# Attention with the softmax's divisor on the diagonal of the turning matrix, values in runs of 512 columns, and the sink as a score column

## The chip, the cores and the metric

The kernel runs on one core of a Trainium2 chip. Its time is the device time of one launch in microseconds (us). Before the change the median of 3 runs was 1434.32 us (1434.02 to 1434.58).

## What is computed

Two layers of a trunk for 128 context tokens and 256 latent tokens of width 1024. Each layer is half a SwiGLU FFN, a mixer, half a SwiGLU FFN, and each part has an RMS norm with shift, scale and gate. Layer 0 mixes by gated linear attention and a Fourier transform. Layer 1, the one that the change touches, mixes by attention with 16 query heads over 4 key/value heads of 64 channels:

```python
def _sink_attend(q, k, v, valid, sink):
    s = jnp.einsum('bqhgd,bkhd->bhgqk', q, k).astype(jnp.float32)
    if valid is not None:
        s = jnp.where(valid, s, -jnp.inf)
    sk = jnp.broadcast_to(sink.astype(jnp.float32)[None, :, :, None, None], s.shape[:-1] + (1,))
    p = jax.nn.softmax(jnp.concatenate([s, sk], axis=-1), axis=-1)[..., :-1]
    return jnp.einsum('bhgqk,bkhd->bqhgd', p.astype(v.dtype), v)
```

Context queries see the 128 context keys. Latent queries see the 128 cached context keys and the latent keys within 128 positions. The sink is one more logit per head: it takes part in the sum of the softmax and has no value.

## The kernel before

Activations lie with channels on the partitions and the 384 tokens along the free axis (128 context, then 256 latent, in two blocks of 128). The large projections are split into a high and a low part and run as three fp32r products each (helpers `mm3x`, lines 352 to 354, and `mm3`, lines 345 to 347); the attention's own products are plain fp32.

In `mixer_swa` the attention is cut into 20 pieces, the list `todo` (line 877). A piece is `(kp, blk, g)`: `kp` is a pair of key/value heads (one on partitions 0 to 63, one on 64 to 127), `blk` a block of 128 tokens (0 context, 1 and 2 latent), `g` one of the four query head pairs. A latent piece is one head pair over 384 keys, 16 of them; a context piece is two head pairs over 128 keys, 4 of them. Tile names carry the piece: `pw013` is `kp` 0, `blk` 1, `g` 3. Each piece goes through four stages:

- `score` (lines 787 to 801): products into one of three double banks of PSUM, `banks`. For latent pieces the band of the window is added by two bf16 products with the identity (line 800).
- `probs` (lines 805 to 828): VectorE takes the maximum over the keys (816), combines it with the negated sink (817) and forms the sink's exponent (819); ScalarE takes the exponentials of each head with their sums (823, helper line 83) and that of the sink (824).
- `scale` (lines 830 to 840): VectorE adds the sink to the sums (833) and takes 1 / sum (836); the probabilities are multiplied by it, half on VectorE and half on GpSimd (840). It runs for a piece when the next piece's `probs` has been issued.
- `turn_probs` and `attend` (lines 842 to 874): six (four for a context piece) 128x128 transposes on TensorE into `banks[0]` (848), a copy to SBUF on ScalarE (850), and the products with the values, twelve instructions of 128 columns for a latent piece (870), four of 256 for a context piece (861). After the fourth head pair the result is split into `hh` and `hl`.

`step(n)` (line 890) sets TensorE's order: the scores of piece n, the turning of piece n - 3, the values of piece n - 4. TensorE's order is written by hand (`manual_schedule`) up to the last piece's scores; the order on VectorE, ScalarE and GpSimd and the tail are set by the tile scheduler. `banks[0]` takes every turning, so one piece's turning can start only when ScalarE has copied the piece before it. Around the pieces stand the rotary embedding of the last query pairs (`rope`, lines 729 to 737, on TensorE, VectorE and GpSimd) and behind them the output projection (`project_out`, lines 345 to 347).

## Time and profile before

| | before |
|---|---|
| median of 3 runs | 1434.32 us |
| the profiled execution | 1434.01 us, its span 1432.2 us |
| TensorE busy | 1405.7 us, 98% of the span |
| VectorE, ScalarE, GpSimd busy | 76%, 42%, 9% |
| share of TensorE in the chain that ended last | 96% |

The page's first part gives busy time by engine; its fourth part follows the work that ended last backwards through what released it. The attention's pieces run between 1045 and 1111 us of the span. TensorE executes every fp32 product of this kernel as two instructions, and a transpose as one; instruction counts in the rows below are those of the hardware.

### The profile page before, as it was taken

What the parts mean: (1) busy time and instruction counts of PE and PEld (TensorE: products, weight loads), DVE (VectorE), ACT (ScalarE), POOL (GpSimd) and SP (SyncE); (2) the same over time, 40 slices, a digit from 0 to 9 for tenths busy, and PEclk for the clock granted to TensorE, in tenths of its full rate; (3) what the DMA queues carried; (4) which work ended last, traced back from release to release, by engine and by line L of the source; (5) the groups of instructions that cost most, each with busy time, mean ns of one, the idle gap of its engine ahead of it and who ended that gap; (6) DMA issues with size and microseconds to landing.
All of it is one profiled execution on the core that took longest, in us unless ns stands there. A gap on an engine that the chain in (4) does not pass through costs nothing.

```text
span 1432.2 us, 21543 instructions
## 1 busy us (share of the span) xinstructions
PE 1405.7 (98%) x8512; PEld 1367.7 (95%) x8512; DVE 1088.3 (76%) x1829; ACT 599.2 (42%) x981; POOL 123.8 (9%) x97
## 2 busy tenths in 40 slices
PE   6999999999999999999999999999999999999996
PEld 5999999999889999999999999999976999999996
DVE  3899989879876888888869988885687676666433
ACT  4544343435344444343344434333357443444332
POOL 2000000102102000000100000010146200000001
PEclk9999999999999999999999999999999999999999
DMA  9666666563414456656646655665420244333331
GB/s 394 253 215 210 213 198 246 204 223 108 155 45 148 143 195 208 203 178 226 214 162 208 213 209 183 204 213 181 146 89 2 103 141 154 136 130 130 121 103 44
DMA packets 48515, 245.26 MB, mean 171 GB/s; under 512 B 5376, under 2 KB 9856, under 8 KB 29088
## 3 DMA queue, kind: packets, MB, share of 16 engines
q1 hardware_dynamic: 44560, 240.80, 48.3%
q10 hardware_dynamic: 3856, 3.10, 0.7%
q8 instruction: 66, 1.08, 0.3%
q14 instruction: 33, 0.27, 0.1%
HBM read 241.79 MB, written 2.10 MB: 170 GB/s over the span
## 4 chain that ended last, share of the span: by engine, by line
PE 96%; DMA 2%; DVE 1%; ACT 0%; issue 0%; SPq 0%; DVEq 0%; ACTq 0%
PE ffn_p L352 17%; PE ffn_p L354 17%; PE ffn_p L353 17%; PE ffn_acc L345 9%; PE ffn_acc L346 9%; PE ffn_acc L347 9%; DMA raw_mod<-in_modw 2%; PE out_acc L345 2%; PE out_acc L347 2%; PE out_acc L346 2%; PE av L870 1%; PE attn L797 1%; PE attn L352 1%; PE attn L848 1%; PE attn L353 1%; PE attn L354 1%
## 5 line engine op out<-in xcount | busy, mean ns | idle before, releaser
L211 ACT CAST whi<-raw 128x1024 fp32r<-128x1024 f32 (+2 forms) x317 | 324.6, 1027 | 606.5 <-PE ffn_p L353 285.5
L212 DVE TENSOR_TENSOR wlo<-raw,whi 128x1024 fp32r<-128x1024 f32 (+2 forms) x317 | 378.6, 1197 | 164.2 <-ACT whi L211 163.4
L352 PE MATMUL ffn_p<-hh,whi 128*128 128x388 f32 x1408 | 478.4, 340 | 3.0 <-ACT whi L211 3.0
L354 PE MATMUL ffn_p<-hh,wlo 128*128 128x386 f32 x1408 | 475.1, 337 | 0.3 <-DVE wlo L212 0.2
L353 PE MATMUL ffn_p<-hl,whi 128*128 128x384 f32 x1408 | 472.5, 336 | 0.0
L149 DVE SCALAR_TENSOR_TENSOR junk<-modw,cb 128x1024 f32<-128x1024 f32 x256 | 314.4, 1228 | 2.1
L352 PEld LDWEIGHTS ffn_p<-hh,whi 128*128 128x128 f32 x1408 | 265.3, 188 | 4.3 <-ACT whi L211 3.3
L354 PEld LDWEIGHTS ffn_p<-hh,wlo 128*128 128x128 f32 x1408 | 265.9, 189 | 1.5 <-DVE wlo L212 1.5
L353 PEld LDWEIGHTS ffn_p<-hl,whi 128*128 128x128 f32 x1408 | 264.8, 188 | 0.5
L345 PE MATMUL ffn_acc<-gh_ffn,whi 128*128 128x384 f32 x704 | 237.0, 337 | 0.8 <-DVE x L400 0.8
L347 PE MATMUL ffn_acc<-gh_ffn,wlo 128*128 128x384 f32 x704 | 236.9, 337 | 0.0
L346 PE MATMUL ffn_acc<-gl_ffn,whi 128*128 128x384 f32 x704 | 236.9, 336 | 0.0
L201 POOL TENSOR_TENSOR ssq_n<-ssq_n,sq_n 128x384 f32<-128x384 f32 x42 | 59.1, 1408 | 891.6 <-ACT sq_n L200 867.3
L345 PEld LDWEIGHTS ffn_acc<-gh_ffn,whi 128*128 128x128 f32 x704 | 132.8, 189 | 1.2 <-DVE x L400 1.2
L347 PEld LDWEIGHTS ffn_acc<-gh_ffn,wlo 128*128 128x128 f32 x704 | 132.7, 189 | 0.0
L346 PEld LDWEIGHTS ffn_acc<-gl_ffn,whi 128*128 128x128 f32 x704 | 132.7, 189 | 0.0
L438 DVE TENSOR_TENSOR ffn_e<-ffn_p,r_n 128x768 f32<-128x768 f32 x88 | 84.0, 955 | 49.0 <-PE ffn_p L354 48.9
L83 ACT ACTIVATE ffn_e<-ffn_e,ffn_wb 128x128 f32<-128x128 f32 (+1 forms) x176 | 70.2, 448 | 55.3 <-DVE ffn_wb L372 55.0
L212 DVE TENSOR_TENSOR gl_ffn<-ffn_e,gh_ffn 128x384 fp32r<-128x384 f32 x88 | 49.0, 557 | 36.4 <-ACT gh_ffn L211 36.2
L211 ACT CAST gh_ffn<-ffn_e 128x384 fp32r<-128x384 f32 x88 | 44.9, 512 | 58.8 <-DVE ffn_e L442 58.3
L442 DVE SCALAR_TENSOR_TENSOR ffn_e<-ffn_e,ffn_wb 128x128 f32<-128x128 f32 (+1 forms) x176 | 65.0, 412 | 0.0
L233 DVE SCALAR_TENSOR_TENSOR hl<-x,mods,hh 128x128 fp32r<-128x128 f32 (+1 forms) x96 | 57.2, 638 | 2.1 <-ACT hh L232 1.3
(260 smaller groups left out, 1251.5 us busy)
## 6 DMA issues: line engine op xcount, KB each, us to landing
raw<-in_w SPq DMA_DIRECT2D x120, 1024.0 KB, 4.8
modw<-in_modw SPq DMA_DIRECT2D x128, 512.0 KB, 3.4
raw<-in_w SPq DMA_DIRECT2D x16, 768.0 KB, 4.9
raw_mod<-in_modw SPq DMA_DIRECT2D x8, 1024.0 KB, 15.7
raw<-in_w_in SPq DMA_DIRECT2D x8, 1024.0 KB, 5.0
raw<-in_w_out SPq DMA_DIRECT2D x8, 1024.0 KB, 4.9
raw<-in_w_og SPq DMA_DIRECT2D x2, 1024.0 KB, 4.8
raw<-in_w_v SPq DMA_DIRECT2D x2, 1024.0 KB, 4.7
```

What stands on the lines that cost most here:

```text
L83: i = act.activation(out, in_, func, **kw)
L149: i = dve.scalar_tensor_tensor(junk, raw, 1.0, cb[:, c], op0=ALU.mult, op1=ALU.mult, accum_out=mods[l][v][:, d, c : c + 1])
L211: i = act.copy(hi, src).ins
L212: pace["last"] = dve.tensor_tensor(lo, src, f(hi), op=ALU.subtract).ins
L345: first = pe.matmul(out, lhsT=wh, rhs=mh, start=start, stop=False)
L346: pe.matmul(out, lhsT=wh, rhs=ml, start=False, stop=False)
L347: pace["product"] = pe.matmul(out, lhsT=wl, rhs=mh, start=False, stop=stop).ins
L352: first = pe.matmul(out[:, :TX], lhsT=wh, rhs=hh[:, k, :TX], start=(k == 0), stop=False)
L353: pe.matmul(out[:, :T], lhsT=wh, rhs=hl[:, k], start=False, stop=False)
L354: pe.matmul(out[:, :TM], lhsT=wl, rhs=hh[:, k, :TM], start=False, stop=(k == KD - 1))
L438: dve.tensor_tensor(e, pp[:, :, :T], feed.r.unsqueeze(1).broadcast_to([P, 2, T]), op=ALU.mult)
L442: dve.scalar_tensor_tensor(e[:, 1, t0:t1], e[:, 1, t0:t1], wb[:, 1, c : c + 1], e[:, 0, t0:t1], op0=ALU.add, op1=ALU.mult)
```

## The change

- The sink, divided by the scale 0.125, is written by VectorE as one more column of the scores in PSUM. The maximum and the exponentials run over 385 (context: 129) columns, so the sum holds the sink; the separate sink exponent, its subtraction and its addition are gone.
- The probabilities are not multiplied by 1 / sum. VectorE writes instead, for each head, a 128x128 matrix with 1 / sum on its diagonal (`inv`), and the transposes with the identity become plain fp32 products with that matrix.
- The turned probabilities of the four head pairs of one `(kp, blk)` are collected in one tile, `[P, 3, 2, 512]` with one buffer, and the values of all four are computed at once: twelve instructions of 512 columns in place of four times twelve of 128.
- In `step`, the values stand ahead of the turning. The scores of the fifth piece are no longer issued ahead of the first turning.

```diff
@@ probs @@
-                    s, w = s[:, :, :T].unsqueeze(1), tile_.unsqueeze(1)
-                sink = nsink[:, 2 * j0 : 2 * (j0 + n)]
+                    s, w = [v_[:, :, : T + 1].unsqueeze(1) for v_ in (s, tile_)]
+                dve.tensor_copy(s[:, :, :, P if blk == 0 else T], sinks[:, 2 * j0 : 2 * (j0 + n)].rearrange("p (g a) -> p g a", g=n))
                 mx = mw.tile([P, 2 * n], F32, tag=f"mx{n}", name=f"mx{nm}", bufs=bufs)
                 dve.reduce_max(mx.rearrange("p (g a) -> p g a", g=n), s, axis=AX.X)
-                dve.scalar_tensor_tensor(mx, mx, -PSC, sink, op0=ALU.mult, op1=ALU.min)
-                es = mw.tile([P, 2 * n], F32, tag=f"es{n}", name=f"es{nm}", bufs=bufs)
-                last = dve.tensor_tensor(es, mx, sink, op=ALU.subtract).ins
+                last = dve.tensor_scalar(mx, mx, -PSC, None, op0=ALU.mult).ins
...
-                actf(es, es, AF.Exp, "exp")
@@ scale @@
-                w, sm, es, n = unscaled.pop(0)
-                i = dve.tensor_tensor(sm, sm, es, op=ALU.add)
+                key, sm, n = unscaled.pop(0)
+                i = dve.reciprocal(sm, sm)
                 if behind:
                     after(i.ins, behind, "the next block's maxima before the sums")
-                dve.reciprocal(sm, sm)
-                for i in range(2 * n):
-                    g, par_ = divmod(i, 2)
-                    e = pool if par_ else dve
-                    e.tensor_scalar(w[:, g, par_], w[:, g, par_], sm[:, i : i + 1], None, op0=ALU.mult)
+                inv[key] = mw.tile([P, 2 * n, P], F32, tag=f"inv{n}", name=f"inv{key[0]}{key[1]}{key[2]}", bufs=4 - n)
+                dve.tensor_tensor(
+                    inv[key], ident.unsqueeze(1).broadcast_to([P, 2 * n, P]), sm.unsqueeze(2).broadcast_to([P, 2 * n, P]), op=ALU.mult
+                )
@@ turn_probs @@
-                        pe.transpose(pt[:, par_, i * P : i * P + P], w[:, par_, i * P : i * P + P], ident)
-                wt = mw.tile([P, 2, T], F32, tag="pT", name=f"pT{nm}")
-                act.copy(wt[:, :, :n], pt[:, :, :n])
+                        pe.matmul(pt[:, par_, i * P : i * P + P], lhsT=w[:, par_, i * step : i * step + P], rhs=inv[kp, blk, g][:, par_ if blk else 2 * i + par_],
+                                  start=True, stop=True, skip_group_check=True)
...
+                if g == 0:
+                    turned[kp, blk] = mw.tile([P, 3, 2, 512], F32, tag="pT", name=f"pT{kp}{blk}", bufs=1)
+                wt = turned[kp, blk]
+                act.copy(wt[:, :, :, g * P : g * P + P], pt[:, :, :n].rearrange("p a (i t) -> p i a t", i=3))
@@ attend @@
+                if blk and g < 3:
+                    return
+                n = 512 if blk else 2 * P
+                po = one_bank(f"av{kp}{blk}{g}")[:, :n]
+                for i, vv in enumerate((vc, vt[:, 1], vt[:, 2]) if blk else (vt[:, 0],)):
                     for par_, rows in enumerate(halves):
                         c0 = (2 * kp + par_) * 64
...
+                        pe.matmul(po[rows], lhsT=vv[:, c0 : c0 + 64], rhs=wt[:, i, par_] if blk else wt[:, par_],
+                                  start=(i == 0), stop=(i == 2 or blk == 0), skip_group_check=True)
@@ step @@
                 if n < len(todo) and n not in ws:
                     begin(n)
+                if 0 <= n - LAG - 1:
+                    attend(*todo[n - LAG - 1], wts_.pop(n - LAG - 1))
                 if 0 <= n - LAG < len(todo):
                     wts_[n - LAG] = turn_probs(*todo[n - LAG], ws[n - LAG])
-                if 0 <= n - LAG - 1:
-                    attend(*todo[n - LAG - 1], wts_.pop(n - LAG - 1))
...
                 queries(3, banks[1], lambda: begin(3))
-                begin(4)
```

Two places show what this does to the order. The first is TensorE in the step of the last piece, 123. Before, it holds the scores of 123 (`kc,qs`) with the band, the transposes of 120 (`ident,pw`) and the 128-column value products of 113 (`av`):

```order
L797 MATMUL attn1_9243<-kc_9010,qs_9161 128x384 x2
L800 LDWEIGHTS c_identb_9008
L800 MATMUL attn1_9243<-c_band_9006,c_identb_9008 128x128
L800 LDWEIGHTS c_identb_9008
L800 MATMUL attn1_9243<-c_band_9006,c_identb_9008 128x128
L848 MATMUL attn0_9242<-ident_75,pw120_9938 128x128 x6
L870 MATMUL av11_9960<-pT113_10023,vc_9011 64x128 x2
L870 MATMUL av11_9960<-pT113_10023,v1_9154 64x128 x4
```

After the change TensorE has in the same step, behind the turning of 113, the scores of 123, the values of the whole group 110 to 113 and the turning of 120 (a row here counts a product once; the hardware runs it as two instructions unless it is a transpose):

```order
L845 MATMUL attn0_9242<-inv113_9850,pw113_9809 128x128 x6
L799 MATMUL attn1_9243<-kc_9010,qs_9161 128x384 x2
L802 LDWEIGHTS c_identb_9008
L802 MATMUL attn1_9243<-c_band_9006,c_identb_9008 128x128
L802 LDWEIGHTS c_identb_9008
L802 MATMUL attn1_9243<-c_band_9006,c_identb_9008 128x128
L869 MATMUL av113_9918<-pT11_9835,vc_9011 64x512 x2
L869 MATMUL av113_9918<-pT11_9835,v1_9154 64x512 x4
L845 MATMUL attn0_9242<-inv120_9872,pw120_9841 128x128 x6
```

The value products have left three steps of four, where only the scores now stand between two turnings, and stand in the fourth as 512 columns ahead of the turning. The second place is ScalarE some 30 us earlier. Before, each piece's copy (`pT`, of the turning in the same step) stands ahead of the exponentials (`pw`) of that step's scores:

```order
L850 COPY pT011_9616<-attn0_9242 128x768
L83 ACTIVATE pw020_9596,sm020_9602<-attn2_9244,mx020_9597 128x384 x2
L83 ACTIVATE es020_9600<-es020_9600 128x2
L850 COPY pT012_9658<-attn0_9242 128x768
L83 ACTIVATE pw100_9636,sm100_9642<-attn1_9243,mx100_9637 128x128 x4
L83 ACTIVATE es100_9640<-es100_9640 128x4
L850 COPY pT013_9692<-attn0_9242 128x768
L83 ACTIVATE pw021_9670,sm021_9676<-attn2_9244,mx021_9671 128x384 x2
```

After the change the exponentials of a step stand ahead of its copy there (the copies into `pT01` are those of pieces 011, 012 and 013 in turn):

```order
L84 ACTIVATE pw020_9575,sm020_9580<-attn2_9244,mx020_9577 128x385 x2
L855 COPY pT01_9569<-attn0_9242 128x6x128
L84 ACTIVATE pw100_9604,sm100_9609<-attn1_9243,mx100_9606 128x129 x4
L855 COPY pT01_9569<-attn0_9242 128x6x128
L84 ACTIVATE pw021_9628,sm021_9633<-attn2_9244,mx021_9630 128x385 x2
L855 COPY pT01_9569<-attn0_9242 128x6x128
L84 ACTIVATE pw022_9657,sm022_9662<-attn1_9243,mx022_9659 128x385 x2
```

The copy that frees `banks[0]` for the next turning now waits in ScalarE's queue behind exponentials of scores that were issued just before the turning that it copies. Over the 16 pieces from 012 on this is so for ten; for 012, 102, 111, 120, 121 and 122 the copy still stands first.

## Rows read from the trace of the kernel before

**Rows 1.** The page: busy time by engine; the chain that ended last, by engine.

```profile
PE 1405.7 (98%) x8512; PEld 1367.7 (95%) x8512; DVE 1088.3 (76%) x1829; ACT 599.2 (42%) x981; POOL 123.8 (9%) x97
...
PE 96%; DMA 2%; DVE 1%; ACT 0%; issue 0%; SPq 0%; DVEq 0%; ACTq 0%
```

**Rows 2.** Windows: length, busy time (instructions) by engine, granted clock, DMA share, GB/s.

```profile
1060.25:1110.50 50.25, 49.06 (x439) 32.24 (x438) 40.32 (x116) 38.99 (x117) 28.81 (x24) 1.00 0.07 22
...
1120.00:1420.00 300.00, 299.17 (x1717) 298.58 (x1716) 169.49 (x260) 120.03 (x176) 18.87 (x13) 1.00 0.35 121
```

**Rows 3.** TensorE by line and shape: count, busy us, mean ns of one.

```profile
L848 PE MATMUL attn<-ident,pw 128*128 128x128 f32 x112 | 15.8, 275 | 0.7 <-ACT pT L850 0.7
...
L870 PE MATMUL av<-pT,v 128*64 128x128 f32 x128 | 9.7, 273 | 0.0
...
L630 PE MATMUL fb<-c_cs_s,fy 128*128 128x128 f32 x32 | 4.2, 276 | 0.0
...
L677 PE MATMUL om<-osq,ones_h 128*128 128x512 f32 x6 | 3.2, 610 | 0.2 <-ACT osq L675 0.2
```

**Rows 4.** Timeline of TensorE, one step: start us, us, instructions.

```profile
1097.82 0.92 PE L797 MATMUL attn<-kc,qs 64*128 64x384 f32 x4
1098.67 0.28 PE L800 MATMUL attn<-c_band,c_identb 128*128 128x128 bf16 x2
1098.79 0.83 PE L848 MATMUL attn<-ident,pw 128*128 128x128 f32 x6
1099.55 0.44 PE L870 MATMUL av<-pT,vc 128*64 128x128 f32 x4
1099.82 0.61 PE L870 MATMUL av<-pT,v 128*64 128x128 f32 x8
1100.36 0.92 PE L797 MATMUL attn<-kc,qs 64*128 64x384 f32 x4
```

**Rows 5.** Timeline of TensorE at other places, layer 0 first.

```profile
387.85 1.05 PE L630 MATMUL fb<-c_cs_s,fy 128*128 128x128 f32 x8
...
406.67 1.02 PE L677 MATMUL om<-osq,ones_h 128*128 128x512 f32 x2
...
1062.58 0.66 PE L848 MATMUL attn<-ident,pw 128*128 128x128 f32 x4 [0.68 <-ACT pT L850]
...
1086.57 0.61 PE L848 MATMUL attn<-ident,pw 128*128 128x128 f32 x4
```

**Rows 6.** Timeline of ScalarE in the step of rows 4.

```profile
1097.87 0.59 ACT L83 ACTIVATE pw<-attn,mx 128x384 f32<-128x384 f32 x1
...
1098.99 0.21 ACT L83 ACTIVATE es<-es 128x2 f32<-128x2 f32 x1
1099.71 0.80 ACT L850 COPY pT<-attn 128x768 f32<-128x768 f32 x1 [0.50 <-PE attn L848]
1100.41 0.59 ACT L83 ACTIVATE pw<-attn,mx 128x384 f32<-128x384 f32 x1
```

**Rows 7.** Timeline of VectorE in the same step.

```profile
1098.99 0.96 DVE L816 TENSOR_REDUCE mx<-attn 128x2 f32<-128x768 f32 x1 [0.45 <-PE attn L800]
1099.98 0.16 DVE L817 SCALAR_TENSOR_TENSOR mx<-mx,nsink 128x2 f32<-128x2 f32 x1
1100.18 0.16 DVE L819 TENSOR_TENSOR es<-mx,nsink 128x2 f32<-128x2 f32 x1
...
1100.45 0.17 DVE L836 RECIPROCAL sm<-sm 128x2 f32<-128x2 f32 x1
1100.66 0.42 DVE L840 TENSOR_SCALAR pw<-pw,sm 128x384 f32<-128x384 f32 x1
```

**Rows 8.** Timeline of VectorE where the pieces begin, and beside the rotary embedding.

```profile
1063.66 0.95 DVE L816 TENSOR_REDUCE mx<-attn 128x2 f32<-128x768 f32 x1
...
1072.35 1.23 DVE L833 TENSOR_TENSOR sm<-sm,es 128x2 f32<-128x2 f32 x1
```

**Rows 9.** Timeline of GpSimd beside the last of rows 8.

```profile
1072.29 1.27 POOL L737 TENSOR_TENSOR qs<-qs,rp2q 128x512 f32<-128x512 f32 x1
```

More of the change, by code (lines that the diff above doesn't have):

```diff
@@ L33 @@
 TH = T + 16
+SK = P + 4
 LAG = 3
@@ L725, in mixer_swa @@
             halves = (slice(0, 64), slice(64, P))
-            nsink = mp.tile([P, 16], F32, name="nsink")
-            dve.tensor_scalar(nsink, pcol("sink"), -1.0, None, op0=ALU.mult)
+            sinks = mp.tile([P, 16], F32, name="sinks")
+            dve.tensor_scalar(sinks, pcol("sink"), 1.0 / PSC, None, op0=ALU.mult)
             def rope(src, dst, nm):
@@ L791, in score @@
                         for par_, rows in enumerate(halves):
-                            pe.matmul(s[:, par_, i * P : i * P + P], lhsT=qs[rows, 4 * kp + g + i, :P], rhs=kr[rows, kp, :P],
+                            pe.matmul(s[:, par_, i * SK : i * SK + P], lhsT=qs[rows, 4 * kp + g + i, :P], rhs=kr[rows, kp, :P],
                                       start=True, stop=True, skip_group_check=True)
@@ L801, in score @@
                               start=False, stop=True, skip_group_check=True)
-            unscaled = []
+            unscaled, inv = [], {}
             def probs(kp, blk, g, s):
@@ L808, in probs @@
                 n, j0, bufs = 1 if blk else 2, 4 * kp + g, LAG + 2
[L809 removed]
+                tile_ = mw.tile([P, 2, T + 4], F32, tag="pw", name=f"pw{nm}", bufs=bufs)
                 if blk == 0:
[L811 removed]
+                    s, w = [v_[:, :, : 2 * SK].rearrange("p a (g k) -> p g a k", g=2)[:, :, :, : P + 1] for v_ in (s, tile_)]
                 else:
[L813 to L814 removed]
+                    s, w = [v_[:, :, : T + 1].unsqueeze(1) for v_ in (s, tile_)]
+                dve.tensor_copy(s[:, :, :, P if blk == 0 else T], sinks[:, 2 * j0 : 2 * (j0 + n)].rearrange("p (g a) -> p g a", g=n))
                 mx = mw.tile([P, 2 * n], F32, tag=f"mx{n}", name=f"mx{nm}", bufs=bufs)
                 dve.reduce_max(mx.rearrange("p (g a) -> p g a", g=n), s, axis=AX.X)
[L817 to L819 removed]
+                last = dve.tensor_scalar(mx, mx, -PSC, None, op0=ALU.mult).ins
                 sm = mw.tile([P, 2 * n], F32, tag=f"sm{n}", name=f"sm{nm}", bufs=bufs)
@@ L842, in turn_probs @@
+                dve.tensor_tensor(
+                    inv[key], ident.unsqueeze(1).broadcast_to([P, 2 * n, P]), sm.unsqueeze(2).broadcast_to([P, 2 * n, P]), op=ALU.mult
+                )
             def turn_probs(kp, blk, g, w):
-                nm = f"{kp}{blk}{g}"
                 pt = banks[0]
-                n = T if blk else 2 * P
+                n, step = (T, P) if blk else (2 * P, SK)
                 for par_ in range(2):
                     for i in range(n // P):
-                        pe.transpose(pt[:, par_, i * P : i * P + P], w[:, par_, i * P : i * P + P], ident)
@@ L849, in turn_probs @@
-                wt = mw.tile([P, 2, T], F32, tag="pT", name=f"pT{nm}")
-                act.copy(wt[:, :, :n], pt[:, :, :n])
+                        pe.matmul(pt[:, par_, i * P : i * P + P], lhsT=w[:, par_, i * step : i * step + P], rhs=inv[kp, blk, g][:, par_ if blk else 2 * i + par_],
+                                  start=True, stop=True, skip_group_check=True)
+                if blk == 0:
+                    wt = mw.tile([P, 2, 2 * P], F32, tag="pT0", name=f"pT{kp}{blk}{g}", bufs=1)
+                    act.copy(wt, pt[:, :, :n])
+                    return wt
@@ L859, in attend @@
                     for par_, rows in enumerate(halves):
                         c0 = (2 * kp + par_) * 64
-                        pe.matmul(po[rows], lhsT=vt[:, 0, c0 : c0 + 64], rhs=wt[:, par_, : 2 * P], start=True, stop=True, skip_group_check=True)
-                    g0 = g
-                else:
-                    if (kp, blk) not in outs:
-                        outs[kp, blk] = one_bank(f"av{kp}{blk}")
-                    po, g0 = outs[kp, blk], 0
-                    for i, vv in enumerate((vc, vt[:, 1], vt[:, 2])):
-                        for par_, rows in enumerate(halves):
-                            c0 = (2 * kp + par_) * 64
-                            pe.matmul(po[rows, g * P : g * P + P], lhsT=vv[:, c0 : c0 + 64], rhs=wt[:, par_, i * P : i * P + P],
-                                      start=(i == 0), stop=(i == 2), skip_group_check=True)
@@ L872, in attend @@
-                if blk == 0 or g == 3:
-                    heads = slice(kp * 4 + g0, kp * 4 + g + (1 if blk else 2))
-                    split(hh[:, heads, ts], hl[:, heads, ts], po.rearrange("p (g t) -> p g t", t=P))
+                        pe.matmul(po[rows], lhsT=vv[:, c0 : c0 + 64], rhs=wt[:, i, par_] if blk else wt[:, par_],
+                                  start=(i == 0), stop=(i == 2 or blk == 0), skip_group_check=True)
+                heads = slice(kp * 4, kp * 4 + 4) if blk else slice(kp * 4 + g, kp * 4 + g + 2)
@@ L876, in mixer_swa @@
+                split(hh[:, heads, ts], hl[:, heads, ts], po.rearrange("p (g t) -> p g t", t=P))
             lat = [(kp, blk, g) for kp in range(2) for blk in (1, 2) for g in range(4)]
```

8 lines of the change are left out of this document (2 added, 6 removed).

## The prediction

> **What bounds the kernel now.** I read the busy times and the chain first: TensorE is busy 98% of the span and holds 96% of the chain that ended last [rows 1]. The windows then say whether that holds where the change is: from the end of the last query projection (1060.25) to the end of the last values (1110.5) TensorE is busy 49.06 of 50.25 us at a granted clock of 1.00 (2.4 GHz), and behind it 299.17 of 300 [rows 2]. So TensorE's work in the attention stands on the path, 1.19 us of waiting is all that other work could give back there, and a later end of the attention moves the end of the kernel by the same amount. VectorE with 40.3 us and ScalarE with 39.0 have slack in the sum, though not much within a step. The timelines of one step give the parts: scores and band 0.97 us, transposes 0.76, values 0.81, together 2.54 from one start of scores to the next [rows 4].
>
> **Turning as a product.** Six transposes take 0.83 us and four 0.61, so one more costs 0.11 [rows 4, 5]. There are 112 instructions [rows 3] for 16 x 6 + 4 x 4 = 112 transposes: one each. A plain fp32 product of the same shape, 128x128 by 128 columns, stands in layer 0 at line 630: the code has 24, the trace has 32 + 16 instructions (the row of the 32 is in [rows 3]), two each, and eight take 1.05 us with 0.28 for one, which is (1.05 - 0.28) / 7 = 0.11 apart [rows 3, 5]. So a turning of a latent piece goes from 6 to 12 instructions 0.11 apart, from 0.76 to 1.42 us to the next block: 112 x 0.11 = +12.3 us on TensorE.
>
> **Values in runs of 512.** Before, six pairs of instructions, one for each half of the partitions, start 0.11 apart: eight instructions take 0.61, which is 3 x 0.11 + 0.27. The block takes 0.81 to the next scores, that is 6 x 0.11 and 0.15 that does not depend on the columns [rows 4]. For 512 columns the nearest rows are two full-width instructions that take 1.02 where one takes 0.61: 0.41 apart [rows 3, 5], about 4 x 0.11, so I take 0.43. A block is then 6 x 0.43 + 0.15 = 2.73, and about 0.1 more since TensorE now goes from the band to the half-width products and from them to the turning (a start behind a change of form comes 0.2 after the last one, not 0.11: 0.76 = 5 x 0.11 + 0.21). Per group 4 x 0.81 = 3.24 becomes 2.83; four groups give -1.6. Bounds: 0.41 a pair and no extra change of form, -2.5; the halves not side by side at 512 columns, 12 x 0.43, +8.7.
>
> The Trainium skill, page "TensorEngine Tiling (Array Packing)", section "Instruction Overhead", says that each matmul carries about 60 cycles of overhead. By it the 144 instructions that go would save 144 x 25 ns = 3.6 us. The trace does not bear it out here: starts 0.11 apart for 128 columns, against 0.41 to 0.43 for 512, leave almost nothing per instruction.
>
> **What goes elsewhere.** VectorE per piece: the exponent's subtraction, the addition and the scaling go (two small instructions of about 0.16 and one of 0.42 [rows 7]); a copy of two sink values and the diagonal (256 columns, bounded by 0.42 for 384) come. That is about even. It runs beside TensorE's step, which grows. ScalarE loses an exponent of two values, some 0.1 to 0.2 per piece. GpSimd loses its scaling, which nobody waited for long. All this I put at nothing while TensorE is the bound; if VectorE's copy to PSUM takes 0.4 instead of 0.2 it enters the waits below.
>
> **The new wait: one bank for the turnings.** A turning may start only when ScalarE has copied the last one. In the step of [rows 4, 6], the last transpose starts at 1099.35 (1098.79 + 5 x 0.11), the copy at 1099.71, and takes 0.80; so from the start of a 12-instruction turning the bank is free again after 11 x 0.11 + 0.36 + 0.80 + 0.05 = 2.44. TensorE comes back to it after 1.42 of turning and 0.97 of scores, 2.39, where values no longer stand between (before: 0.76 + 0.81 + 0.97 = 2.54 against 1.77). So the cover shrinks from 0.8 us to nothing, and a bank wait of this kind has a precedent: 0.68 at 1062.58, where two turnings followed each other [rows 5].
>
> It is worse where the exponentials stand ahead of the copy in ScalarE's queue. From a start of scores: maximum at +1.17 (1098.99 against 1097.82), here +1.37 behind the sink's copy; 0.99 to the next instruction, 0.20 until its result is used, two exponentials 1.12 (1097.87 to 1098.99), the copy 0.80, and 0.05: 4.53 [rows 4, 6, 7]. TensorE wants the bank at 0.97 + 2.39 = 3.36, so it is 1.2 late. The next such piece then starts its scores late enough to find its exponentials ready, so the loss falls on about every second one. I walked the order given for the two engines:
> - before the turning of 011: 1.7. VectorE is busy with the last query projection until 1063.66 [rows 8], and the maxima of 012 and 013 queue behind it.
> - before 013: 1.2, and up to 1.0 more, since VectorE stood still beside GpSimd's rotary product there (a sum of two columns took 1.23, to 1073.58, where GpSimd's 1.27 from 1072.29 ends) [rows 8, 9] and the maximum of 100 is scaled at that place.
> - before 100, 022 and 102: 0.4, 0.3, 0.9; the values of group 02 wait 0.2; the pieces from 111 on, whose copy stands first, 0.05 each, 0.3.
> - before 020, 021, 023, 110 and 120 none: values stand between scores and turning.
> Sum 5.0 without the rope's 1.0. That is the value taken; its ends are 0, if ScalarE's order costs nothing, and 10, if each of the ten pieces loses about a microsecond.
>
> **Sum.** +12.3 - 1.6 - 1.2 (the old waiting, whose causes are priced anew) + 5.0 = +14.5. The profiled execution took 1434.01, its span and 1.8 around it, 0.3 below the median of the runs; 1434.0 + 14.5 gives 1448.5.
>
> **Rivals.**
> - *The copies stay hidden.* Only TensorE's own work counts: +12.3 - 1.6 - 1.2 = +9.5, 1443.5. For it: ScalarE and VectorE are under 80% busy in [rows 2]. Against it: 2.44 against 2.39 leaves no cover at all.
> - *The wait grows into the bound.* Each piece with exponentials first loses its microsecond: +9.5 + 10 = +19.5, 1453.5. For it: rope and split casts on both queues; against it: the alternation above and six pieces with the copy first.
> - *512 columns break the overlap of the halves.* -1.6 becomes +8.7: 1458. Nothing in the trace shows 512 at half width; 128 columns, and the scores' 384 (four in 0.92 [rows 4], where serial ones would take over 1.2), do overlap.
> - *The product costs TensorE no more than the transpose.* Then +12.3 and most of the waits fall: -1.6 - 1.2, 1431, faster. It decides if two instructions together start 0.12 apart or less. Line 630's eight in 1.05 us speak against it, as they are the same shape and type.
> - *It costs four times a transpose.* 112 x 3 x 0.11 = +37, and the copies hidden behind it: 1434 + 37.3 - 1.6 - 1.2 = 1468.5. Against it the same rows: 0.22 a product. The Trainium skill, "TensorE: Matmul & The Clock Gate", section "Terms", gives the transpose mode as 4x faster for FP32; by that rule this rival would hold, and line 630 says 2x.
>
> **How the numbers follow.** Forecast 0.62 (its own range 1445.5 to 1451.5), hidden copies 0.17, larger wait 0.16, no overlap 0.02, free product 0.02, fourfold product 0.01. The range of 8 in 10 is from 1442.5, the hidden copies with the cheaper bound of the values (0.9 less), to 1453.5, the larger wait. Beyond 0.2% (2.9 us), about what a measurement of this kernel can tell from no change, only the free product could come near the other side: -2.8 is at the edge, so I split its 0.02. Faster 0.01, same 0.01, slower 0.98.
>
> **What would show it.** In the profile after: 224 turning instructions 0.11 apart and 1.42 per latent turning (wrong at 0.76, or far above 1.6); 48 value instructions with pairs about 0.43 apart, 2.7 to 2.9 a block; TensorE idle ahead of turnings, released by ScalarE's copy, 4 to 7 us in all, the longest ahead of 011 and 013 and little from 111 on; no loss before 1060 or behind the attention. The prediction is wrong if TensorE's busy time in the attention grows by less than 8 us, if the waits stay under 2 or go over 9, or if they name VectorE's diagonal in place of the copy.

## The result, and the profile after

The changed kernel takes 1451.53 us in the median of 4 runs (1451.48 to 1451.58), against 1434.34 before on the same chip: ratio 1.0121 [1.0108, 1.0134], 17.2 us slower. The forecast of 1448.5 was 3 us short: inside the range of 8 in 10 (1442.5 to 1453.5), and 0.03 us above the end of the narrower range that the forecast had for itself (1445.5 to 1451.5). The profiled execution took 1451.58 with a span of 1449.8, against 1434.01 and 1432.2, so the spans differ by 17.6.

From the page after, the busy times and the chain that ended last, which answer to [rows 1]:

```profile
PE 1419.8 (98%) x8480; PEld 1376.4 (95%) x8480; DVE 1085.1 (75%) x1805; ACT 598.2 (41%) x961; POOL 95.7 (7%) x73
...
PE 94%; DVE 2%; DMA 2%; ACT 1%; issue 0%; SPq 0%; DVEq 0%; ACTq 0%
```

TensorE is busy 14.1 us longer and idle 30.0 us of the span in place of 26.5. These two, 14.1 and 3.5, are the whole 17.6. VectorE and GpSimd have less work than before, and it buys nothing.

A total over the whole kernel holds one thing that no edit touched. In the first 40 us, where TensorE stands still for a third of the time, it is busy 26.49 us before, 26.24 after, and up to 27.61 in the traces of the experiments; what it is busy more there it is idle less. So the totals scatter by up to 1.4 us, and work is better compared from 1040 us on. The line before, and the one after:

```profile
1040.00:1432.20 392.20, 380.10 (x2337) 359.49 (x2336) 237.89 (x431) 173.72 (x335) 58.23 (x45) 0.99 0.31 105
1040.00:1449.80 409.80, 394.50 (x2305) 368.17 (x2303) 235.49 (x407) 172.56 (x315) 29.82 (x21) 0.99 0.29 101
```

Counted so, TensorE's work grows by 14.4 us and its idle time by 3.2.

Windows of the kernel after (length, busy time by engine with instructions, granted clock, DMA share, GB/s). The first two answer to [rows 2], the other three are one stretch inside the attention:

```profile
1060.25:1128.00 67.75, 63.16 (x410) 42.85 (x408) 37.91 (x97) 38.74 (x105) 5.08 (x4) 0.97 0.05 16
1130.00:1438.00 308.00, 307.17 (x1760) 305.63 (x1757) 173.12 (x266) 122.73 (x180) 19.28 (x13) 1.00 0.34 118
...
1075.60:1077.40 1.80, 0.03 (x1) 0.00 (x0) 1.66 (x6) 1.80 (x9) 0.00 (x0) 1.00 0.00 0
1077.40:1080.50 3.10, 3.04 (x14) 2.96 (x15) 0.44 (x1) 1.37 (x6) 0.00 (x0) 0.54 0.00 0
1080.50:1082.50 2.00, 2.00 (x10) 0.99 (x8) 0.69 (x1) 0.57 (x1) 0.85 (x1) 0.86 0.00 0
```

The attention takes 67.75 us against 50.25, and what follows runs as full as before: a plain shift. (The two stretches don't hold quite the same work: the new one ends ahead of the last values, which start at 1128.26, and holds some 23 products of the output projection where the old one holds 9. The two differences nearly cancel.) Inside, TensorE waits 4.59 us against 1.19. And there is something that the prediction did not have: after a stretch of 1.8 us with 0.03 us of work, the granted clock reads 0.54, close to the lower of its two levels (1.2 GHz of 2.4), and then 0.86 on the way back. In narrower windows the clock reads 1.00 to the end of the idle stretch and until 1077.60, when TensorE had just taken up work again, and 0.51 from there to 1081.00.

TensorE's timeline after (start us, us, instructions, and idle time before with its releaser), which answers to [rows 4]; the lines left out repeat the pattern:

```profile
1063.83 1.16 PE L845 MATMUL attn<-inv,pw 128*128 128x128 f32 x8
1064.91 0.92 PE L799 MATMUL attn<-kc,qs 64*128 64x384 f32 x4
...
1066.56 1.60 PE L845 MATMUL attn<-inv,pw 128*128 128x128 f32 x12
1068.10 0.92 PE L799 MATMUL attn<-kc,qs 64*128 64x384 f32 x4
...
1069.92 1.60 PE L845 MATMUL attn<-inv,pw 128*128 128x128 f32 x12 [0.69 <-ACT pT L855]
1071.36 1.03 PE L735 MATMUL rotq<-qs,c_rot 128*128 128x256 f32 x4
...
1075.35 0.28 PE L802 MATMUL attn<-c_band,c_identb 128*128 128x128 bf16 x2
1077.46 2.78 PE L845 MATMUL attn<-inv,pw 128*128 128x128 f32 x12 [1.82 <-ACT pT L855]
1080.03 1.54 PE L735 MATMUL rotq<-qs,c_rot 128*128 128x256 f32 x4
...
1082.57 1.08 PE L869 MATMUL av<-pT,vc 128*64 128x512 f32 x4
1083.47 1.89 PE L869 MATMUL av<-pT,v 128*64 128x512 f32 x8
1085.29 0.94 PE L845 MATMUL attn<-inv,pw 128*128 128x128 f32 x6
```

A latent turning has 12 instructions and takes 1.54 to the next block (1066.56 to 1068.10) where 0.76 stood before; a context turning takes 1.08 (1063.83 to 1064.91). The values block of 512 columns takes 2.72 (1082.57 to 1085.29). One turning, at 1077.46, took 2.78 with the same 12 instructions, and the rotary product behind it 1.54 where the one at 1071.36 took 1.03.

Why TensorE stood for 1.82 us there is read from the other engines. ScalarE's timeline after, around that place:

```profile
1075.21 0.37 ACT L84 ACTIVATE pw<-attn,mx 128x129 f32<-128x129 f32 x1 [2.56 <-DVE sm L832]
...
1076.60 0.81 ACT L855 COPY pT<-attn 128x768 f32<-128x768 f32 x1
```

VectorE's timeline in the same stretch, and under it GpSimd's:

```profile
1074.03 1.09 DVE L819 TENSOR_SCALAR mx<-mx 128x4 f32<-128x4 f32 x1
1075.03 0.15 DVE L832 RECIPROCAL sm<-sm 128x2 f32<-128x2 f32 x1
```

```profile
1073.82 1.27 POOL L739 TENSOR_TENSOR qs<-qs,rp2q 128x512 f32<-128x512 f32 x1
```

The copy that frees the turning bank (1076.60) stands behind the exponentials of piece 100; those waited for VectorE, whose scaling of four maxima took 1.09 us, where the same instruction took 0.17 at 1088.52, and ended at about 1075.1, where GpSimd's 1.27 from 1073.82 end too. (The profile names the reciprocal right behind the scaling as the releaser; the exponentials read only the maxima.) ScalarE was idle for 2.56 us, and from about 1074.5, when the turning ahead had ended, with a copy to do that its queue held back.

The waits of TensorE in the attention after (tile and line that waited, releaser: us in all, times, longest) name that copy but for one of 0.5 us, as the prediction said, and no scores:

```profile
PE attn L845 <- ACT pT L855: 3.6, 5, 1.8
PE attn L845 <- ACT pw L84: 0.5, 1, 0.5
PE av L869 <- ACT pT L855: 0.4, 1, 0.4
```

### The profile page after: what moved, and what is told of

Its sections match the earlier page's. It is cut to its first block, busy times and chain, and to the rows that moved or that the text cites. A ratio compares the mean times of both kernels' runs of the same rounds, so it can differ in the third digit from the quotient of the medians.

```text
span 1449.8 us, 21341 instructions
## 1 busy us (share of the span) xinstructions
PE 1419.8 (98%) x8480; PEld 1376.4 (95%) x8480; DVE 1085.1 (75%) x1805; ACT 598.2 (41%) x961; POOL 95.7 (7%) x73
## 3 DMA queue, kind: packets, MB, share of 16 engines
q8 instruction: 66, 1.08, 0.3%
## 4 chain that ended last, share of the span: by engine, by line
PE 94%; DVE 2%; DMA 2%; ACT 1%; issue 0%; SPq 0%; DVEq 0%; ACTq 0%
PE ffn_p L353 17%; PE ffn_p L355 17%; PE ffn_p L354 17%; PE ffn_acc L347 8%; PE ffn_acc L346 8%; PE ffn_acc L348 8%; DMA raw_mod<-in_modw 2%; PE out_acc L346 2%; PE out_acc L348 2%; PE out_acc L347 2%; PE attn L845 1%; PE av L869 1%; ACT pw L84 1%; DVE mx L818 1%; PE attn L799 0%; PE fa L623 0%
```

## The experiments

Unless it says otherwise, a ratio is to the kernel before, run on the same chip between the others. The chips differ a little: on them the kernel before took 1434.05 to 1434.48 us, so two versions are best compared by what each takes beyond its own kernel before. "The change" is the kernel of the section above.

**The product alone.** The kernel before with the diagonal matrix as the only edit:

```diff
-                for i in range(2 * n):
-                    e.tensor_scalar(w[:, g, par_], w[:, g, par_], sm[:, i : i + 1], None, op0=ALU.mult)
+                dve.tensor_tensor(inv[key], ident.unsqueeze(1)..., sm.unsqueeze(2)..., op=ALU.mult)
...
-                        pe.transpose(pt[...], w[...], ident)
+                        pe.matmul(pt[...], lhsT=w[...], rhs=inv[kp, blk, g][...], start=True, stop=True, skip_group_check=True)
```

> The kernel before with one part of the change: the transposes become fp32 products with the diagonal of 1 / sum; values by piece, the separate sink and the step's order stay as before. Theory (TensorE's own work is the cost; a turning goes from 0.76 to 1.54 us for a latent piece and from 0.54 to 1.09 for a context piece, as the profile after the change shows): 16 x 0.78 + 4 x 0.55 = +14.7 on TensorE, and as values still stand between two turnings the bank is free in time, so the waits for ScalarE's copy stay under 1.5 us in the attention and the granted clock stays at 1.00: 1447.5 to 1449.5 us. Rival (the new order of values and turnings is what costs, not the product): under 1441 us.

Measured 1449.07 us (1448.94 to 1449.16), ratio 1.0102 [1.0085, 1.0118]. TensorE's busy time is 1420.9, 15.2 more than before, of which 0.9 falls into the first 40 us; from 1040 us on it is 394.43, 14.3 more. On cost the theory holds; the rival that the order is what costs, and that of a free product, are dead. The granted clock reads 1.00 in the attention, as expected. The waits for the copy, expected under 1.5 us, were larger:

```profile
PE attn L848 <- ACT pT L851: 2.3, 4, 1.0
```

**The transposes back.** The change with the scaling and the transposes of before, and the values and the sink as changed:

```diff
-                inv[key] = mw.tile([P, 2 * n, P], F32, ...)
-                dve.tensor_tensor(inv[key], ...)
+                for i in range(2 * n):
+                    g, par_ = divmod(i, 2)
+                    e = pool if par_ else dve
+                    e.tensor_scalar(key[:, g, par_, ...], key[:, g, par_, ...], sm[:, i : i + 1], None, op0=ALU.mult)
...
-                        pe.matmul(pt[...], lhsT=w[...], rhs=inv[kp, blk, g][...], ...)
+                        pe.transpose(pt[...], w[...], ident)
```

> The changed kernel with one part undone: transposes with the identity, and the scaling by 1 / sum on VectorE and GpSimd, as before; values in runs of 512, the sink as a column and the new order stay. Theory (the product costs TensorE 14.7 us): that falls away, but TensorE then comes back to the one bank of the turnings after 0.76 + 0.97 = 1.73 us where it is free after 1.77 at best, and later behind exponentials, so the waits grow from 4.6 us to 6 to 10 us and eat the 1.6 us that the runs of 512 save: 1435 to 1440 us, not faster than before. Rival (runs of 512 and the sink's column are a gain once the product is gone): 1431 to 1433 us.

Measured 1435.22 us (1435.14 to 1435.62), ratio 1.0007 [0.9998, 1.0017]. It takes 1.0 us more than its own kernel before, so 16.2 of the 17.2 us go with the product. TensorE has 1.4 us less work than before (1404.3 busy; 1.6 less from 1040 us on) and more waits:

```profile
PE attn L799 <- ACT pw L84: 2.0, 5, 0.8
PE attn L845 <- ACT pT L854: 1.1, 1, 1.1
PE attn L845 <- ACT pw L84: 0.7, 1, 0.7
```

The saving of the runs of 512 is there and is given back: 2.0 us of these 3.8 are scores that wait for a bank whose exponentials are late, a wait that the change does not show, and that the slower turning probably covers there. Not all of it comes from the runs: the longest, 0.80 at 1067.12, has its like in the kernel with the sink column alone (below), 0.99 at 1067.44.

**The copy first.** The change with the exponentials of a step issued behind its turning:

```diff
-                ws[n] = probs(*todo[n], s)
+                return lambda: ws.update({n: probs(*todo[n], s)})
...
-                if n < len(todo) and n not in ws:
-                    begin(n)
+                then = begin(n) if n < len(todo) and n not in ws else None
...
                     wts_[n - LAG] = turn_probs(*todo[n - LAG], ws[n - LAG])
+                if then:
+                    then()
```

> The changed kernel with the exponentials of a step issued behind the turning of the same step, so that ScalarE's copy stands ahead of them in its queue; TensorE's order and all instructions are the same. Theory (TensorE waits for the bank of the turnings because the copy queues behind exponentials, and the longest wait lets the clock fall): the waits before 011, 013, 022 and 102, 0.7, 1.8, 0.6 and 0.2 us, fall to 0.3 or less each, the clock stays at 1.00 in the attention: 1446 to 1448 us. Rival (VectorE and ScalarE cannot deliver faster, whatever stands first): the waits come back under other names, 1450 us or more.

Measured 1446.61 us (1446.39 to 1446.76), ratio 1.0085 [1.0070, 1.0100]: 12.4 us more than its own kernel before, where the change takes 17.2 more. Its waits, and then its timeline of TensorE at the turning that took 2.78 us in the change:

```profile
PE attn L845 <- ACT pT L855: 1.1, 2, 0.8
PE attn L845 <- ACT pw L84: 0.5, 1, 0.5
```

```profile
1075.40 1.60 PE L845 MATMUL attn<-inv,pw 128*128 128x128 f32 x12 [0.77 <-ACT pT L855]
1076.84 1.03 PE L735 MATMUL rotq<-qs,c_rot 128*128 128x256 f32 x4
```

The wait is 0.77 and the turning takes 1.60 again; the granted clock reads 1.00 in every 10 us of the attention. Waits fell from 4.6 to 1.6, which is 3.0 us, and TensorE's busy time from 1040 us on fell by 2.1 (392.38 against 394.50), close to what the slow stretch cost. The order on ScalarE makes most of the waits, as the prediction had it. The 0.77 is more than the 0.3 that I expected to be left: one of the four exponentials of piece 100 still stands ahead of the copy in ScalarE's timeline (1074.20, the copy at 1074.56), and it waited for the same VectorE scaling of 1.09 us.

**Values by piece.** The change with 128-column values after each piece, still ahead of the turning:

```diff
-                if blk and g < 3:
-                    return
-                n = 512 if blk else 2 * P
-                po = one_bank(f"av{kp}{blk}{g}")[:, :n]
+                n = P if blk else 2 * P
+                if blk == 0:
+                    po = one_bank(f"av{kp}{blk}{g}")[:, :n]
+                else:
+                    if g == 0:
+                        outs[kp, blk] = one_bank(f"av{kp}{blk}")
+                    po = outs[kp, blk]
+                at_ = slice(g * P, g * P + P) if blk else slice(0, n)
...
-                        pe.matmul(po[rows], lhsT=..., rhs=wt[:, i, par_] ...
+                        pe.matmul(po[rows, at_], lhsT=..., rhs=wt[:, i, par_, at_] ...
...
+                if blk and g < 3:
+                    return
```

> The changed kernel with the values computed piece by piece in runs of 128 columns again, at the place in the step that they have after the change (ahead of the turning); the diagonal product and the sink's column stay. Theory (runs of 512 save 1.6 us of TensorE but uncover the bank's copy): TensorE's work grows by 1.6 us, the waits of 4.6 us fall to 2 or less and the half clock (some 1.7 us) goes: 1447 to 1449.5 us, faster than the whole change. Rival (the runs of 512 are a plain gain): 1453 us.

Measured 1452.47 us (1452.43 to 1452.49), ratio 1.0126 [1.0110, 1.0141]: a miss, on the rival's side. I had taken the values for a cover of the copy. Placed ahead of the turning they need the very copy that the turning waits for, since they read what it writes. TensorE's timeline of this kernel shows the wait in its new place:

```profile
1078.27 0.44 PE L873 MATMUL av<-pT,vc 128*64 128x128 f32 x4 [1.03 <-ACT pT L855]
...
1079.07 1.60 PE L845 MATMUL attn<-inv,pw 128*128 128x128 f32 x12
```

Its waits sum to 4.3 us, nearly those of the change, now ahead of the values. The longest is 1.03, and the clock reads 1.00 throughout. TensorE's busy time from 1040 us on is 395.49; against the change without its slow stretch (394.50 - 1.7, below) that is 2.7 more, and against the kernel with the copy first, which has no slow stretch, 3.1: nearly twice the 1.6 that I had for the runs of 512.

**Transposes and the copy first.** The two edits above together.

> The change with the four transposes and the scaling of the probabilities as they were before (1435.22 us as measured), and in each step the exps issued behind the step's turning, so that the copy out of the turning bank stands first on ScalarE. In the kernel without this reordering TensorE waits 1.1 us once in front of a turning for such a copy, 0.7 us once for exps that still read the turning bank, and 2.0 us in five places in front of scores for exps that still read their bank. Theory (the waits for the copy come from ScalarE's order): the 1.1 us go, the scores' waits stay or grow a little because every exp starts up to one copy (0.8 us) later: 1433.8 to 1435.4 us. Rival (without the dearer product there is no slack on TensorE to cover exps that start 0.8 us later, so the scores' five waits each grow): 1436 us or more.

Measured 1435.34 us (1435.14 to 1437.88), ratio 1.0006 [0.9997, 1.0015]. The number lies in the theory's range, but the run doesn't test it, because the tile scheduler, which orders ScalarE, put the exponentials ahead of the copy again. ScalarE's timeline of this kernel, at the place:

```profile
1072.99 0.37 ACT L84 ACTIVATE pw<-attn,mx 128x129 f32<-128x129 f32 x1 [0.65 <-DVE sm L832]
...
1074.38 0.81 ACT L854 COPY pT<-attn 128x768 f32<-128x768 f32 x1
```

The waits are the same three lines with the same numbers as without the edit. Inconclusive: here the order of issue was only a wish, since a scheduler decides.

**Runs of 512 alone.** The kernel before with the values of four pairs collected, turning ahead of values as before:

```diff
-                wt = mw.tile([P, 2, T], F32, tag="pT", name=f"pT{nm}")
-                act.copy(wt[:, :, :n], pt[:, :, :n])
...
+                if g == 0:
+                    turned[kp, blk] = mw.tile([P, 3, 2, 512], F32, tag="pT", name=f"pT{kp}{blk}", bufs=1)
+                wt = turned[kp, blk]
+                act.copy(wt[:, :, :, g * P : g * P + P], pt[:, :, :n].rearrange("p a (i t) -> p i a t", i=3))
...
+                    if g < 3:
+                        return
...
-                            pe.matmul(po[rows, g * P : g * P + P], lhsT=..., rhs=wt[:, par_, i * P : i * P + P],
+                            pe.matmul(po[rows], lhsT=..., rhs=wt[:, i, par_],
```

> The kernel before with one part of the change alone: values of four head pairs in one run of 512 columns, the turning ahead of the values as before, transposes and sink as before. Theory (TensorE loses 16 x 6 instruction gaps and three changes of form per group and waits for nothing new): 1.0 to 1.8 us faster, 1432.4 to 1433.3 us. Rival 1 (the one buffer for four pairs makes the first copy of a group wait for the 2.7 us of values of the group before, which now stand behind that turning, and the next turning waits for that copy, at three changes of group, about 0.7 us each): 1434 to 1436 us. Rival 2 (what was seen in the kernel with 128-column values, 3.6 us more work of TensorE, belongs to the block of 512 everywhere): 1430.5 to 1431.3 us.

Measured 1437.94 us (1437.43 to 1439.43), ratio 1.0026 [1.0015, 1.0036]: 3.5 slower, above all three ranges. The work did what the theory says (1404.2 busy, 1.5 less). Its waits in the attention:

```profile
PE attn L797 <- ACT pw L83: 1.8, 3, 1.0
PE attn L848 <- ACT pT L857: 1.7, 1, 1.7
PE attn L848 <- DVE pw L840: 1.2, 1, 1.2
PE attn L848 <- POOL pw L840: 0.8, 2, 0.5
PE attn L848 <- ACT pT L851: 0.7, 1, 0.7
```

6.2 us against 1.2 before, minus 1.5 of work, is the 3.5. The waits are of four kinds, and in this trace the single buffer of rival 1 is a small part of them at most. ScalarE's timeline at the longest, 1.66 ahead of a turning at 1082.46:

```profile
1080.39 0.58 ACT L83 ACTIVATE pw<-attn,mx 128x384 f32<-128x384 f32 x1 [2.85 <-DVE mx L817]
...
1081.61 0.80 ACT L857 COPY pT<-attn 128x768 f32<-128x768 f32 x1
```

The values that held the buffer had given it back before 1080.2; the copy started at 1081.61 because exponentials stood ahead of it. (Whether the scheduler would have put the copy first with a second buffer, no run shows.) The rest are probabilities scaled late and scores that wait for exponentials. My reading, which no run isolates, is that three steps in a row without values are shorter than VectorE and ScalarE need for a piece.

**The sink column alone.** The kernel before with the sink as a column, by the edits of `probs` and the first lines of `scale` in the diff of the change, with the layout that they need, nothing else.

> The kernel before with the sink as one more column of the scores alone: per block a copy of the sinks into the score bank (0.16 us on VectorE), the max over one column more, no exp and no sum of the sink. Theory (none of this stands on TensorE, and exps start about as late as before): within 0.6 us of before, 1433.6 to 1434.9 us. Rival (the sink's copy cannot start before the scores are written and puts 0.16 us ahead of each max, so exps and everything behind them move, 20 blocks x 0.1 to 0.16 us): 1435.5 to 1437 us.

Measured 1434.87 us (1434.42 to 1436.74), ratio 1.0005 [0.9996, 1.0014]: no difference that can be measured, as expected; TensorE's busy time is the same 1405.7. Its trace is not the same, though: scores wait 1.3 us for exponentials (0.2 before), 0.99 of it once, and the waits of TensorE in the attention sum to 2.2 us against 1.1.

**Transposes in the old order.** Values and sink as changed, transposes and scaling as before, and the order of before:

```diff
-                if 0 <= n - LAG - 1:
-                    attend(*todo[n - LAG - 1], wts_.pop(n - LAG - 1))
                 if 0 <= n - LAG < len(todo):
                     wts_[n - LAG] = turn_probs(*todo[n - LAG], ws[n - LAG])
+                if 0 <= n - LAG - 1:
+                    attend(*todo[n - LAG - 1], wts_.pop(n - LAG - 1))
...
                 queries(3, banks[1], lambda: begin(3))
+                begin(4)
```

> Values in runs of 512 and the sink column as in the change, with the four transposes, the scaling and the order of before (turning, then values; piece 4 begun ahead of the loop). It differs from the measured 1435.22 us by the order alone. Theory (the order of the change, values ahead of the turning, costs what the runs of 512 save, through waits in front of scores and turnings): 1432.0 to 1433.5 us, waits of TensorE in the attention under 2.5 us against 3.8. Rival (the single buffer of four pairs holds the first copy of the next group until the values behind the turning have run): 1434.5 to 1436 us.

Measured 1434.87 us (1434.53 to 1436.34), ratio 1.0002 [0.9993, 1.0011], above the theory's range. Its waits sum to 4.4 us, not under 2.5, of which the largest line is again scores behind exponentials (0.99 of it at the place of the wait in the kernel with the sink column alone):

```profile
PE attn L799 <- ACT pw L84: 3.0, 4, 1.2
```

With 1435.22 for the other order the order of turning and values makes no difference that can be measured here. The theory that it costs what the runs of 512 save falls.

**Filler in the wait.** The change with 14 transposes of the identity ahead of the one turning that waited 1.82 us:

```diff
+                if n - LAG == 5:
+                    fill = one_bank("fill")
+                    for _ in range(14):
+                        pe.transpose(fill[:, :P], ident, ident)
                 if 0 <= n - LAG < len(todo):
```

> The change, with 14 transposes of the identity (128x128, into a bank of their own that nobody reads) put on TensorE ahead of the turning of piece 013, in front of which TensorE waited 1.82 us in the change; at the 0.11 us that one transpose took in the trace of before they fill 1.5 us of that wait. Theory (the turning that took 2.78 us instead of 1.60, and the product behind it that took 1.54 instead of 1.03, ran slowly because the granted clock fell to 0.54 after the wait): with the wait filled the granted clock stays at 1.00 there, the turning takes 1.6 us, and the kernel is 1.4 to 1.9 us faster than the change, 1449.6 to 1450.2 us. Rival (that turning is slow for a reason of its own, its operands or its bank, and the clock reading follows from it): the turning again takes over 2.5 us, and the time is that of the change or up to 0.3 us more, 1451.4 to 1451.9 us.

Measured 1449.99 us (1449.70 to 1451.71), ratio 1.0114 [1.0098, 1.0129]: 1.5 less than the change, or 1.3 when each is set against its own kernel before (15.9 and 17.2 more), with more work in it. One of the four executions took 1451.71, as long as the change; its trace was not kept. TensorE's timeline of this kernel, and its windows over the stretches shown for the change:

```profile
1075.51 1.70 PE L897 MATMUL fill<-ident 128*128 128x128 f32 x14
1077.49 1.60 PE L845 MATMUL attn<-inv,pw 128*128 128x128 f32 x12 [0.28 <-ACT pT L855]
1078.93 1.03 PE L735 MATMUL rotq<-qs,c_rot 128*128 128x256 f32 x4
```

```profile
1075.60:1077.40 1.80, 1.61 (x16) 1.37 (x13) 1.66 (x6) 1.80 (x10) 0.00 (x0) 1.00 0.00 0
1077.40:1080.50 3.10, 3.01 (x20) 2.32 (x20) 0.91 (x2) 1.97 (x6) 0.46 (x1) 1.00 0.00 0
```

The turning starts 0.03 us later than in the change, waits for the same copy, has the same operands, and takes 1.60 in place of 2.78. At this place the theory holds: with the same wait filled, the clock stays and the turning is fast. But a wait of nearly that length need not bring the clock down. The kernels with runs of 512 alone and of 256 alone have waits of 1.66 and 1.52 us; their windows over the wait and over the work behind it:

```profile
1080.80:1082.40 1.60, 0.01 (x1) 0.00 (x0) 1.02 (x2) 1.60 (x7) 1.47 (x1) 1.00 0.00 0
1082.40:1085.50 3.10, 3.04 (x22) 1.78 (x24) 2.40 (x7) 2.80 (x13) 1.18 (x1) 1.00 0.01 3
```

```profile
1080.00:1081.50 1.50, 0.00 (x0) 0.00 (x0) 1.32 (x6) 1.28 (x6) 0.85 (x2) 1.00 0.00 0
1081.50:1084.50 3.00, 2.55 (x18) 1.29 (x18) 2.49 (x8) 2.60 (x13) 1.78 (x2) 1.00 0.01 3
```

What sets these apart from the wait of 1.82 us, the runs don't show.

**Runs of 256 alone.** The kernel before with values of two pairs in one run, two buffers. The diff is against the runs of 512 alone:

```diff
-                    turned[kp, blk] = mw.tile([P, 3, 2, 512], ..., bufs=1)
+                    turned[kp, blk] = mw.tile([P, 3, 2, 2 * P], ..., bufs=2)
...
-                    if g < 3:
+                    if g % 2 == 0:
                         return
```

> The kernel before with the values of two head pairs in one run of 256 columns in place of four in 512; two buffers for the turned probabilities of two pairs each. Theory (runs of 512 cost the kernel before 3.5 us although TensorE's work falls by 1.5, because the values come in a lump: three steps without values are shorter than ScalarE and VectorE need for a step, and a single buffer held the next copy): with half the lump and two buffers most of the waits go, TensorE's work falls by 0.8 to 1.1 us against before, the waits of TensorE in the attention stay under 2 us: 1433.2 to 1434.6 us. Rival (any run longer than 128 columns delays the copies by its length and makes waits of the size of the runs of 512): 1436 us or more.

Measured 1435.05 us (1434.79 to 1435.77), ratio 1.0006 [0.9997, 1.0015], between the two expectations. The waits are 3.5 us, where I had under 2. TensorE's busy time is 1405.2, only 0.5 less than before, but the first 40 us hold 0.85 more; from 1040 us on it falls by 1.3, somewhat more than the 0.8 to 1.1 expected:

```profile
1040.00:1433.20 393.20, 378.81 (x2242) 355.24 (x2240) 239.07 (x431) 173.68 (x335) 58.30 (x45) 0.99 0.31 105
```

Half the lump makes about half of the added waiting, which fits the theory; buffer and lump were changed together and are not told apart.

## Why the prediction was right, and where its sizes were off

- **The bound.** TensorE's work and waits in the attention are the whole difference, and nothing before or behind moves: right.
- **Turning as a product, +12.3.** Right in kind, too small by 2.4: the mis-sized term. Twelve instructions take 1.54 to the next block, not 1.42, so 16 x (1.54 - 0.76) = 12.5, and 4 x (1.08 - 0.54) = 2.2 for the context turnings: 14.7 (14.3 of busy time from 1040 us on with the product alone). The prediction multiplied the spacing by the instructions added and kept the start of the block as it was for a transpose. Of 1.54, eleven spacings of 0.11 are 1.21, and 0.33 stand around them; with six transposes it was 0.21 [rows 4]. The Trainium skill, page "TensorE: Matmul & The Clock Gate", section "Terms", puts transposes at 4x the speed for FP32; the measured 0.76 and 1.54 say 2x, so the rival of the fourfold product was rightly given 0.01.
- **Runs of 512, -1.6.** Measured -1.5 of TensorE's busy time from 1040 us on for the runs alone and -1.6 with the sink and the new order, and the block took 2.72 against 2.73 forecast. Right there. In the old order with the sink it was -2.5, and between the change and 128 columns per piece 2.7 to 3.1, so the term depends on its neighbours. The Trainium skill, page "TensorEngine Tiling (Array Packing)", section "Instruction Overhead", has about 60 cycles of overhead for each matmul. An estimate from it is 3.6 for the 144 instructions that go; the kernel with the runs alone shows 1.5, less than half of it.
- **Other engines, 0.** Right for the time of the sink column alone, which can't be told from before, though its trace has 1.1 us more of waits. Not right where the longest wait came from: VectorE's 1.09 us beside GpSimd's rotary product stand on its path. The prediction had seen this and left it out of its sum, as up to 1.0 more ahead of 013.
- **Old waits -1.2, new ones +5.0.** Measured 4.59 in all, from the places foreseen: 011 (0.69 of the 1.7), 013 (1.82, from 1.2 to 2.2), 100, 022, 102 and values 02 (0.30, 0.60, 0.20, 0.43), none from 111 on. A wait of 0.55 ahead of the first turning was not foreseen; there the bank still held scores of 011 that were not yet exponentiated. The mechanism is right, as the copy issued first shows; that the sum came within 0.4 us of the forecast is in part luck, since 011 and 102 were put too high by 1.0 and 0.7, and 013, 022, the values and the first turning too low by 0.6, 0.3, 0.2 and 0.55.
- **The clock, not in the sum.** The prediction took 2.4 GHz for granted, as [rows 2] show 1.00. Behind the 1.82 us wait the clock fell, and the stretch lost about 1.7: (2.78 - 1.60) + (1.54 - 1.03). The filler gives 1.3 to 1.5 of it back, measured.
- **Slips that change next to nothing.** By the prediction's own terms the bank is free after 2.42, not 2.44, which takes about 0.1 off the forecast (the pieces from 111 on); the rival of the halves comes to 1458.8, not 1458; and the rival of the fourfold product adds 37.0 in one place and 37.3 in another. The last two don't stand in the forecast.

Together, from 1040 us on: turning 14.2 of busy time (14.4 + 1.5 - 1.7), runs -1.5, clock 1.7, waits 3.2: 17.6, against 12.3 - 1.6 + 3.8 forecast. (The 14.2 is what the other terms leave, so the sum closes of itself; the kernel with the product alone gives 14.3 by another way.) Turning and clock, 1.9 and 1.7, are the 3 us that were missing; the waits came out 0.6 lower. The parts don't add up as times: alone the product costs 14.9, the runs 3.5 and the sink 0.4 (within its noise), 18.8 together, and the whole costs 17.2, although it holds a loss to the clock that none of the parts has. I read this as the slow turning covering part of the waits that runs and sink make, and no run isolates it: scores that wait for exponentials, 1.8 to 3.0 us in the kernels with runs of 512 and transposes and 1.3 with the sink alone, are not among the waits of the change. No version that was run beats the kernel before; what came nearest does TensorE's work in 1.4 us less and waits for it elsewhere.

Open: which part of the 0.33 around the products is their first spacing and which a change of form; and how far the runs of 512 would pay if VectorE and ScalarE kept up, since no kernel was run in which both were quick enough.

## What to carry to other kernels

Folding a scaling into a transpose makes a plain fp32 product of it, which on the engine that sets the time cost twice the transposes here (1.54 against 0.76 us), whatever it saves on engines that wait. Lumping work saves TensorE a little per instruction, but empties the steps between, and the engines that feed it then show as waits: price the emptiest step and not the mean. Where a forecast contains a wait of a microsecond or two on TensorE, allow for the granted clock behind it as well: one of 1.82 us cost about 1.7 more in that way, one of 1.66 in another kernel nothing.

## What the runs showed of the hardware that was not expected

- One wait of 1.82 us on TensorE was followed by a granted clock of 0.54 over 3.1 us and of 0.86 over the next 2. With 14 transposes in the same place it stayed at 1.00, and waits of 0.77, 1.03, 1.52 and 1.66 us in four other kernels were followed by no fall. The Trainium skill, page "TensorE: Matmul & The Clock Gate", section "🔬 Part 4: PE-mode transpose", says that transposes do not count as work for the clock in the way that products do; the trace differs, since with nothing but transposes in the wait the clock stayed at the higher level, where without them it fell.
- A VectorE operation on four columns took 1.09 us beside a GpSimd product over 512 columns, and ended within 0.05 us of it (1075.12 and 1075.09). The kernel before has two of the kind: 1.23 beside 1.27 [rows 8, 9], and at 1078.65 another sum of two columns in 1.25 beside GpSimd's 1.28 from 1078.60. The one after stands on the path of the 1.82 us wait of TensorE.
